# One masked product for the exponents of a decay matrix, in place of two products added in PSUM

## The chip, the cores and the metric

The kernel runs on one core of a Trainium2 chip. Its time is the device time of one execution in microseconds; the result is told as the median of several runs. TensorE (PE) multiplies matrices into PSUM, VectorE (DVE) and ScalarE (ACT) work element by element, GpSimd (POOL) and SyncE (SP) mostly issue DMAs. Each engine works through its own queue in order.

## What is computed

One layer of a hybrid trunk on 512 latent and 256 context tokens of width 2048: a modulated norm, one input projection, a Fourier head group beside a bidirectional state-space scan of 24 heads (four groups of six), an output projection and an MLP. The change touches the scan. Cut to it, the reference does this for each direction, chunk of 128 positions and head:

```python
acum = jnp.cumsum(dtc * a, axis=2)
seg = acum[:, :, :, None] - acum[:, :, None, :]
decay = jnp.exp(jnp.where(lower, seg, -jnp.inf))
cb = jnp.einsum('bclgn,bcsgn->bclsg', cc, bc)
y_diag = jnp.einsum('bclsgh,bcsghp->bclghp', decay * cb[..., None], xdt)
```

`seg` is the decay's exponent for a pair of positions l and s of one chunk: a term of l less a term of s.

## The kernel before

Everything lies in SBUF as 128 partitions by columns. Products of weights are made in three pieces (`mm3`, lines 106 to 108): a weight tile of 1024 columns is loaded by SP's queue, rounded to a high part by ScalarE (line 99), the rest is taken by VectorE (line 100), and high and low parts multiply 512 moving columns. Two such pairs of tiles (`whi`, `wlo`) exist.

The work goes in stages. Up to 153 us the first slab of the input projection runs beside the adaLN sums, whose weights come through five `araw` buffers. Then the set-up of the scan follows in the same stretch as the first group's projections: `dt_finish` makes the step sizes `dt`, `dta`, and lines 363 to 395 make from `dta` the cumulative sums that the scan needs, in two parts (a rounded one and its rest) so that products keep the precision. `pre` holds the sums for the factors of the states, `prm` the sums for the positions l (56 rows: head, and head again for the rest), and `pch` those for the positions s (112 rows: chunk and head, twice). The scratch tiles `scr` and `hs_` are taken from `araw`. `sel` and `selp` are constants that pick heads; they are loaded and cast after the first group's projections (lines 513 to 516).

Then come the Fourier group, the context tokens (to about 476 us), and from there to about 820 us the scan, `scan_group` four times. In each group `i` goes over three pairs of heads; one such pass is called a unit below, so there are twelve. A unit makes the states (line 631, then VectorE at 640), and for each of its two heads and two directions the exponents: `sg` gets the product of `sel` for the head with `prm` (line 654, 56 rows) and on top of it the product of `pch` with `sel` for the chunk (line 656, 112 rows). ScalarE turns it by Relu and Exp (lines 660, 661) into the decay, VectorE multiplies by B and C's product (662), and PE multiplies with x (667). The states' part follows with `selp` and `pre` (673, 675, 679 to 681), and at the end the gate, whose squares are ScalarE's (588, 591). Beside the units PE works on the projections of the next group (`lat_group`), for the last group on a part of z (`z_last`) and on the output projection.

What stands in which place of each queue is decided when the program is built: a scheduler takes the code's order, priorities (`load_split` has a high one) and free buffers, and writes a fixed order for each engine.

Of the kernel before, what the change touches and what calls it, by code (L numbers as in the profile page):

```python
# [14 lines left out]
P = 128  # L15
# [18 lines left out]
NSB = 14  # L34
SHARED = [(16 + k, 0) for k in range(2, 14)]
NZ1 = 9
N1P = 3
N1S = 2 * N1P

# [15 lines left out]
def tile_hybrid_trunk(ctx, tc, xT, ctxT, cvec, ccol, vec, alog, w_ada, w_adr, w_ins, w_zs, w_in, w_dt, w_f, w_o,  # L55
# [81 lines left out]
    def vcol(i):  # L137
        return vt[:, i:i + 1]
# [77 lines left out]
    na = smp.tile([P, 2 * NH], F32, name="na")  # L216


    pre = smp.tile([56, 2, L], F32R, name="pre")
    prm = smp.tile([56, 2, L], F32R, name="prm")  # L220
    pch = smp.tile([112, 2, 2, P], F32R, name="pch")
    sel = smp.tile([112, 72], F32R, name="sel")
    selp = smp.tile([56, 12, P], F32R, name="selp")

    w_stack = ExitStack()
    open_weights(w_stack, 3, 2)
# [69 lines left out]
    with tc.tile_pool(name="st", bufs=1, side="right") as st, tc.tile_pool(name="st2", bufs=2, side="right") as st2, \  # L296
            tc.tile_pool(name="st4", bufs=3, side="right") as st4:
        cl = st.tile([P, 2 * HALF], F32, name="cl")
        xr = st.tile([P, KT, L], F32, name="xr")

        def ada_k(k):
            for ch in (16 + k, k):
                for hf in range(2):
                    if (ch, hf) in SHARED:
                        ada_half(ara, ch, hf, (mod, part, cl), (modc, partc, ccl))
                    else:
                        ada_half(ara, ch, hf, (mod, part, cl))
# [24 lines left out]
        widths = [P, P, P, P, 48, P, P, P]  # L332
        for k in range(KT):
            w = raw_tile()[:, :SLAB_IN]
            nc.sync.dma_start(out=w, in_=w_ins[k])
            if k == 1:
                nc.sync.dma_start(out=cstt, in_=cst)
                nc.sync.dma_start(out=na, in_=alog)
            hi, lo = big_pair()
            xs_h.append((hi, lo))  # L340
            tmp = st4.tile([P, L], F32, name="mtmp")
            v.tensor_mul(xr[:, k], xr[:, k], rstd)
            s.activation(tmp, xr[:, k], AF.Identity, bias=mod[:, k:k + 1], scale=s1[:, k:k + 1])
            s.copy(hi, tmp)
            o = 0
            for a, n in zip(accs, widths):
                te.matmul(a[:n], w[:, o:o + n], tmp, start=k == 0, stop=k == KT - 1)  # L347
                o += n
            if k + 1 < KT:
                ada_k(k + 1)  # L350
            v.tensor_sub(lo, tmp, hi.bitcast(F32))
        xm = xs_h
        background(6)
        for i in range(4):
            u = st2.tile([P, L], F32, name="sr")
# [10 lines left out]
        v.memset(scr[:, :896], 0.0)  # L366
        hs_ = ara.tile([P, HALF], F32, name="araw").bitcast(F32R)
        lp = scr[:, 0:448].rearrange("p (d c h) -> p d c h", d=2, c=NCH)
        lc = scr[:, 448:896].rearrange("p (d f h) -> p d f h", d=2, f=2)
        for d in range(2):  # L370
            mask = k_le if d == 0 else k_ge
            for o in (0, 32):
                v.tensor_copy(lp[:, d, :, o:o + NH], dta[:, :NCH, d * NH:(d + 1) * NH])
            for f in range(2):
                for o in (0, 64):
                    v.tensor_copy(lc[:, d, f, o:o + 48].rearrange("p (c h) -> p c h", c=NCH),
                                  dta[:, :NCH, d * NH + f * 12:d * NH + f * 12 + 12])
            mid = scr[:, 896:1024]
            v.tensor_scalar(mid, mask, mask[:, 63 + d:64 + d], None, ALU.subtract)
            for dst, m in ((pre, mask), (prm, mid)):  # L380
                pp = bank()
                for c in range(NCH):
                    te.matmul(pp[:56, c * P:(c + 1) * P], lp[:, d, c], m, start=True, stop=True)
                hi = hs_[:, d * L:(d + 1) * L]
                s.copy(dst[0:32, d], pp[0:32, :])
                s.copy(hi[32:56], pp[32:56, :])
                v.tensor_sub(dst[32:56, d], pp[32:56, :], hi[32:56].bitcast(F32))
# [3 lines left out]
            hi = hs_[:, d * L:d * L + 2 * P]  # L391
            po = pch[:, d].rearrange("p f s -> p (f s)")
            s.copy(po[0:64], pg[0:64])
            s.copy(hi[64:112], pg[64:112])
            v.tensor_sub(po[64:112], pg[64:112], hi[64:112].bitcast(F32))

    gp_stack = ExitStack()
    gp1 = gp_stack.enter_context(tc.tile_pool(name="gp1", bufs=1, side="right"))
# [106 lines left out]
    with tc.tile_pool(name="fp", bufs=1, side="right") as fp, tc.tile_pool(name="fp2", bufs=1, side="right") as fp2:  # L505
        tb = fp.tile([P, 8, NL], F32, name="tb")
        cw = fp.tile([P, 2, P], F32, name="cw")
        wf = fp.tile([P, 4, P], F32, name="wf")
        nc.gpsimd.dma_start(out=cw, in_=cw_d)
        nc.gpsimd.dma_start(out=wf, in_=w_f)  # L510
        nc.gpsimd.dma_start(out=tb, in_=dft)
        nxt = lat_group(0, 4, ctx_stats)
        selr = raw_tile()[:112, :72]
        nc.sync.dma_start(out=selr, in_=sel_d)
        s.copy(sel, selr)
        s.copy(selp.rearrange("p j (h q) -> p (j h) q", q=64), selr[:56, :NH].unsqueeze(2).broadcast_to([56, NH, 64]))
# [89 lines left out]
    def scan_group(g, bT, b_tok, cT, xT_, x_tok):  # L606
# [13 lines left out]
        for i in range(3):  # L620
# [29 lines left out]
            for hh in range(2):  # L650
                h = h0 + hh
                for d in range(2):
                    sg = bank()
                    te.matmul(sg, sel[:56, h:h + 1].broadcast_to([56, P]), prm[:, d], start=True, stop=False)
                    j = 24 + (h % 12) * NCH
                    te.matmul(sg, pch[:, d, h // 12], sel[:, j:j + NCH].unsqueeze(2).broadcast_to([112, NCH, P]),
                              start=False, stop=True)
                    e = spe.tile([P, NCH, P], F32, name=f"e{d}")
                    ef = e.rearrange("p a b -> p (a b)")
                    s.activation(ef, sg, AF.Relu, scale=-1.0)  # L660
                    s.activation(ef, ef, AF.Exp, scale=-1.0)
                    v.tensor_mul(e, e, cbu if d == 0 else cbl)
                    ms.append(e)
# [470 lines left out]
```

## Time and profile before

| | |
|---|---|
| median of three runs | 2385.83 us (2382.52 to 2394.14) |
| the profiled execution | 2374.16 us, its span 2372.4 us |
| PE busy | 2262.6 us, 95% of the span |
| DVE busy | 1811.1 us, 76% |
| ACT busy | 1176.3 us, 50% |
| POOL busy | 285.7 us, 12% |

The span goes from the first instruction to the last. Busy shares are averages over stages with different limits, so the stage of the change is to be read by itself. Matmuls are pipelined: the busy time of one reaches into the next, and the distance of their starts tells what one costs in the queue. PEld is the load of the stationary operand, which may lie beside a running product. A wait names who ended the idle time of an engine.

### The profile page before, as it was taken

To read this page: it belongs to the slowest core of one execution; us is meant where nothing else is said; L and a number is where in the kernel's file an instruction comes from. 1 tells how busy PE (TensorE), PEld (TensorE's weight loads), DVE (VectorE), ACT (ScalarE), POOL (GpSimd) and SP (SyncE) were. 2 spreads that over 40 slices of the span, in tenths; PEclk is the share of its full clock that TensorE was granted. 3 is DMA by queue.
4 is the path that set the end of the run, shared out by engine and by line. 5 is a ranking of instruction groups with operands and counts; after the bars stand their busy time and mean duration, and the time that the engine had idled before them with its cause. 6 is when DMAs were issued, how large, how long until landed. Compare 5 with 4: busy or idle time off the path is not lost.

```text
span 2372.4 us, 38829 instructions
## 1 busy us (share of the span) xinstructions
PE 2262.6 (95%) x15242; PEld 2004.8 (85%) x15242; DVE 1811.1 (76%) x2551; ACT 1176.3 (50%) x1646; POOL 285.7 (12%) x375
## 2 busy tenths in 40 slices
PE   6999999999999999898999999999999999999996
PEld 2347789877777777698999989999999999999995
DVE  7978779987778677675666666666898887888778
ACT  4125245456555422254444545555665665566554
POOL 0000000000000000111101101111122222222210
PEclk9999999999999999999999999999999999999998
DMA  8988877823224499557888877777899999999993
GB/s 297 333 296 299 330 240 261 279 83 122 83 63 148 144 345 303 187 163 230 253 224 244 239 217 220 208 209 213 242 264 267 266 250 267 259 265 247 242 267 116
DMA packets 163456, 544.72 MB, mean 230 GB/s; under 512 B 19284, under 2 KB 20196, under 8 KB 163016
## 3 DMA queue, kind: packets, MB, share of 16 engines
q1 hardware_dynamic: 115624, 402.35, 49.6%
q0 software_dynamic: 46496, 137.79, 27.1%
q8 instruction: 119, 1.95, 0.3%
q10 hardware_dynamic: 1152, 2.10, 0.2%
q14 instruction: 65, 0.53, 0.1%
HBM read 479.24 MB, written 62.92 MB: 229 GB/s over the span
## 4 chain that ended last, share of the span: by engine, by line
PE 63%; DVE 15%; DMA 14%; issue 4%; ACT 3%; SPq 0%; DVEq 0%; POOL 0%; ACTq 0%; POOLq 0%
PE acc L107 10%; PE acc L108 10%; PE acc L106 9%; PE bank L107 8%; PE bank L106 8%; PE bank L108 8%; DMA araw<-in_w_ada_dram 5%; DMA wraw<-in_w_adr_dram 3%; DVE araw L172 3%; DVE wlo L100 2%; DVE wlo L85 2%; DMA araw<-in_w_adr_dram 2%; DMA wraw<-in_w_o_dram 1%; PE bank L347 1%; PE bank L667 1%
## 5 line engine op out<-in xcount | busy, mean ns | idle before, releaser
L85 DVE TENSOR_TENSOR wlo<-wraw,whi 128x1024 fp32r<-128x1024 f32 x427 | 519.4, 1221 | 224.0 <-ACT whi L84 221.1
L84 ACT CAST whi<-wraw 128x1024 fp32r<-128x1024 f32 x427 | 445.4, 1048 | 448.8 <-PE bank L108 158.4
L107 PE MATMUL bank<-chi,wlo 128*128 128x256 f32 (+1 forms) x2000 | 569.7, 285 | 6.1 <-DVE wlo L85 6.1
L106 PE MATMUL bank<-chi,whi 128*128 128x256 f32 (+1 forms) x2000 | 569.6, 285 | 1.1 <-DVE ca L1023 0.8
L108 PE MATMUL bank<-clo,whi 128*128 128x256 f32 (+1 forms) x2000 | 569.3, 285 | 0.0
L107 PE MATMUL acc<-chi,wlo 128*128 128x256 f32 (+1 forms) x1512 | 435.7, 288 | 21.7 <-DVE wlo L85 21.5
L106 PE MATMUL acc<-chi,whi 128*128 128x256 f32 (+1 forms) x1512 | 433.4, 287 | 7.3 <-ACT chi L830 6.7
L108 PE MATMUL acc<-clo,whi 128*128 128x256 f32 (+1 forms) x1512 | 433.7, 287 | 0.0
L107 PEld LDWEIGHTS bank<-chi,wlo 128*128 128x128 f32 x2000 | 384.5, 192 | 7.7 <-DVE wlo L85 6.7
L106 PEld LDWEIGHTS bank<-chi,whi 128*128 128x128 f32 x2000 | 384.5, 192 | 2.6 <-DVE ca L1023 1.3
L108 PEld LDWEIGHTS bank<-clo,whi 128*128 128x128 f32 x2000 | 384.5, 192 | 0.9
L107 PEld LDWEIGHTS acc<-chi,wlo 128*128 128x128 f32 x1512 | 293.6, 194 | 25.7 <-DVE wlo L85 24.3
L106 PEld LDWEIGHTS acc<-chi,whi 128*128 128x128 f32 x1512 | 293.1, 194 | 9.5 <-ACT chi L830 7.6
L107 PE MATMUL acc<-bh,wlo 128*128 128x512 f32 x720 | 286.2, 397 | 13.3 <-DVE wlo L100 13.3
L108 PEld LDWEIGHTS acc<-clo,whi 128*128 128x128 f32 x1512 | 293.5, 194 | 1.6 <-DVE clo L832 0.6
L106 PE MATMUL acc<-bh,whi 128*128 128x512 f32 x720 | 285.3, 397 | 1.1 <-ACT whi L99 1.1
L108 PE MATMUL acc<-bl,whi 128*128 128x512 f32 x720 | 284.4, 395 | 0.0
L99 ACT CAST whi<-wraw 128x1024 fp32r<-128x1024 f32 (+2 forms) x145 | 142.7, 987 | 263.3 <-PE acc L108 228.6
L867 POOL DMA_DIRECT2D wraw<-in_w_dram x122 | 105.1, 861 | 757.1 <-DMA wraw<-in_w_dram 334.8
L100 DVE TENSOR_TENSOR wlo<-wraw,whi 128x1024 fp32r<-128x1024 f32 (+2 forms) x145 | 165.6, 1144 | 29.0 <-ACT whi L99 28.0
L107 PEld LDWEIGHTS acc<-bh,wlo 128*128 128x128 f32 x720 | 136.1, 189 | 48.2 <-DVE wlo L100 20.1
L106 PEld LDWEIGHTS acc<-bh,whi 128*128 128x128 f32 x720 | 136.0, 189 | 29.8 <-ACT whi L99 1.6
(336 smaller groups left out, 3274.0 us busy)
## 6 DMA issues: line engine op xcount, KB each, us to landing
wraw<-in_w_dram SPq DMA_DIRECT2D x305, 512.0 KB, 5.2
araw<-in_w_ada_dram SPq DMA_DIRECT2D x164, 512.0 KB, 6.7
wraw<-in_w_dram POOLq DMA_DIRECT2D x122, 512.0 KB, 8.0
wraw<-in_w_in_dram SPq DMA_DIRECT2D x84, 512.0 KB, 4.5
x<-ca POOLq DMA_DIRECT2D x112, 256.0 KB, 8.0
araw<-in_w_adr_dram SPq DMA_DIRECT2D x48, 512.0 KB, 4.6
wraw<-in_w_adr_dram SPq DMA_DIRECT2D x32, 512.0 KB, 7.7
hid<-ct POOLq DMA_DIRECT2D x32, 512.0 KB, 5.4
```

Of the source, the lines that this page charges most:

```text
L84: s.copy(hi, raw)
L85: v.tensor_sub(lo, raw, hi.bitcast(F32))
L99: s.copy(hi, raw)
L100: v.tensor_sub(lo, raw, hi.bitcast(F32))
L106: te.matmul(ps, a[0], b[0], start=first, stop=False, skip_group_check=on)
L107: te.matmul(ps, a[1], b[0], start=False, stop=False, skip_group_check=on)
L108: te.matmul(ps, a[0], b[1], start=False, stop=last, skip_group_check=on)
L172: v.tensor_tensor_reduce(o, a, cond[:, hf * HALF:(hf + 1) * HALF], 1.0, last if hf else first, ALU.mult, ALU.add, dst[:, ch:ch + 1] if hf ...
L347: te.matmul(a[:n], w[:, o:o + n], tmp, start=k == 0, stop=k == KT - 1)
L667: te.matmul(py[hh * 64:hh * 64 + 64, c * P:(c + 1) * P], xd[d][:, c, hh], ms[2 * hh + d][:, c], start=c == 0 and d == 0, stop=c == NCH - 1 ...
L867: nc.gpsimd.dma_start(out=raw[n], in_=d, accum_op=ALU.add)
```

## The change

The two products become one of 128 rows. Its moving operand `mov` (128 x 512 for each direction and each twelve heads) holds the sums of the positions l for the twelve heads, in two parts, in rows 0 to 23, zeros up to row 31, and in rows 32 to 127 ones where a row's chunk is the column's. Its stationary operand has ones in the first 32 rows and the sums of the positions s in the other 96 (`sta`). For each head ScalarE multiplies `sta` by a column of `pick` that has 1, -1 or 0 per row and so leaves the rows of that head alone; that is the masked operand `sh`, of which there are two buffers. `prm` and `pch` go. `selp` goes too, and the 56 x 128 operand of line 673 is spread from `sel` in each unit (`two`). The constants are loaded in the set-up, through `araw`, and the set-up holds a second scratch tile `scr2`.

```diff
-            for dst, m in ((pre, mask), (prm, mid)):
-                pp = bank()
-                for c in range(NCH):
-                    te.matmul(pp[:56, c * P:(c + 1) * P], lp[:, d, c], m, start=True, stop=True)
...
             pg = bank()[:, :2 * P]
             for f in range(2):
-                te.matmul(pg[:112, f * P:(f + 1) * P], lc[:, d, f], mid, start=True, stop=True)
...
+                pm = bank()
+                for c in range(NCH):
+                    te.matmul(pm[:24, c * P:(c + 1) * P], lq[:, d, f, c], mid, start=True, stop=True)
+                s.copy(hi[:24], pm[:24])
+                v.scalar_tensor_tensor(mov[:24, d, f], hi[:24].bitcast(F32), pick[:24, 12:13], pm[:24],
+                                       ALU.mult, ALU.add)
+                te.matmul(pg[:, f * P:(f + 1) * P], lc[:, d, f], mid, start=True, stop=True)
+            s.copy(hi[:, :2 * P], pg)
...
+            s.copy(sta[:32, d], ones[:32].unsqueeze(1).broadcast_to([32, 2, P]))
...
+        selr = ara.tile([P, HALF], F32, name="araw")
+        nc.sync.dma_start(out=selr[:, :NSEL], in_=sel_d)
+        v.tensor_copy(pick[:, 0:13], selr[:, 24:37])
+        s.copy(mov.rearrange("p d f t -> p (d f) t"), selr[:, 37:NSEL].unsqueeze(1).broadcast_to([P, 4, L]))
+        s.copy(sel, selr[:56, :NH])
...
                     sg = bank()
-                    te.matmul(sg, sel[:56, h:h + 1].broadcast_to([56, P]), prm[:, d], start=True, stop=False)
-                    j = 24 + (h % 12) * NCH
-                    te.matmul(sg, pch[:, d, h // 12], sel[:, j:j + NCH].unsqueeze(2).broadcast_to([112, NCH, P]),
-                              start=False, stop=True)
+                    sh = sp2.tile([P, P], F32R, name="sh")
+                    s.activation(sh, sta[:, d, h // 12].bitcast(F32), AF.Copy, scale=pick[:, h % 12:h % 12 + 1])
+                    te.matmul(sg, sh, mov[:, d, h // 12], start=True, stop=True)
...
+            two = sp.tile([56, P], F32R, name="two")
+            s.copy(two.rearrange("p (h q) -> p h q", q=64),
+                   sel[:, h0:h0 + 2].bitcast(F32).unsqueeze(2).broadcast_to([56, 2, 64]))
             for d in range(2):
                 pb = bank()
-                te.matmul(pb, selp[:, g * 3 + i], pre[:, d], start=True, stop=True)
+                te.matmul(pb, two, pre[:, d], start=True, stop=True)
```

The scheduler also writes another order. Three places follow. The lines of the new program are some 10 to 15 higher: its line 667 is the new product, 666 the Copy that makes `sh`, 670 and 671 are Relu and Exp, 107 to 109 are `mm3`.

PE's queue in the third unit of the first group before, from the states' products on:

```order
L631 MATMUL bank<-xs,b_tok 128x128 x3
L654 MATMUL bank<-prm,sel 128x512
L656 MATMUL bank<-sel,pch 128x512
L654 MATMUL bank<-prm,sel 128x512
L656 MATMUL bank<-sel,pch 128x512
L654 MATMUL bank<-prm,sel 128x512
L656 MATMUL bank<-sel,pch 128x512
L654 MATMUL bank<-prm,sel 128x512
L656 MATMUL bank<-sel,pch 128x512
L106 MATMUL acc<-bh,whi 128x512
```

The same place in the new program, its beginning, and then the end of the 21 weight products that follow:

```order
L642 MATMUL bank<-xs,b_tok 128x128 x3
L667 MATMUL bank<-mov,sh 128x512 x2
L108 MATMUL acc<-bh,wlo 128x512
```

```order
L107 MATMUL acc<-bh,whi 128x512
L667 MATMUL bank<-mov,sh 128x512 x2
L677 MATMUL bank<-e_3969,xd_3947 64x128
L686 MATMUL bank<-pre,two 128x512
L692 MATMUL bank<-cT,hg 128x128
```

Eight products in a row have become two, then 21 weight products, then two.

ScalarE's queue in the same unit before (`e` are the decays), from the cast of the weight tile on:

```order
L99 CAST whi<-wraw 128x1024
L464 COPY cvr<-acc 128x512
L660 ACTIVATE e_3934<-bank 128x512
L660 ACTIVATE e_3941<-bank 128x512
L661 ACTIVATE e_3934<-e_3934 128x512
L661 ACTIVATE e_3941<-e_3941 128x512
L660 ACTIVATE e_3948<-bank 128x512
L660 ACTIVATE e_3955<-bank 128x512
```

And in the new program:

```order
L602 ACTIVATE ee<-xT_1184 128x512
L481 ACTIVATE xT_4296<-cvr,vt 128x512
L670 ACTIVATE e_3969<-bank 128x512
L670 ACTIVATE e_3977<-bank 128x512
L100 CAST whi<-wraw 128x1024
L671 ACT_TABLE_LOAD
L671 ACTIVATE e_3969<-e_3969 128x512
L671 ACTIVATE e_3977<-e_3977 128x512
L666 ACTIVATE sh<-sta,pick 128x128 x2
L670 ACTIVATE e_3985<-bank 128x512
```

The two `sh` for the unit's second head stand behind Relu, a weight cast, a table load and Exp of its first.

SP's queue in the set-up before:

```order
L98 DMA wraw<-in_w_in_dram 128x1024 x2
L168 DMA araw<-in_w_ada_dram 128x1024 x3
L98 DMA wraw<-in_w_in_dram 128x1024 x3
L168 DMA araw<-in_w_ada_dram 128x1024 x3
L410 DMA araw<-in_ctxT_dram 128x1024 x3
```

And in the new program:

```order
L99 DMA wraw<-in_w_in_dram 128x1024 x2
L169 DMA araw<-in_w_ada_dram 128x1024 x3
L368 DMA araw<-in_sel_d_dram 128x549
L99 DMA wraw<-in_w_in_dram 128x1024 x3
L169 DMA araw<-in_w_ada_dram 128x1024 x3
L425 DMA araw<-in_ctxT_dram 128x1024 x3
```

The load of the constants has moved from behind the first group's projections to the middle of the set-up.

## Rows read from the trace of the kernel before

**Rows 1.** Waits of PE, 480 to 800 us: total us, times, longest.
```profile
PE bank L610 <- ACT cT L476: 3.0, 3, 1.6
PE bank L631 <- DVE xs L627: 1.0, 1, 1.0
PE acc L107 <- DVE wlo L100: 0.3, 1, 0.3
```
**Rows 2.** Busy time of each engine by stretch: the scan, then the output projection.
```profile
core 0: us, PE busy (x) PEld busy (x) DVE busy (x) ACT busy (x) POOL busy (x), PEclk, DMA share, GB/s
458.00:820.00 362.00, 355.95 (x1864) 269.10 (x1863) 284.49 (x516) 196.15 (x283) 22.91 (x42) 0.99 0.34 106
...
820.00:1000.00 180.00, 163.16 (x698) 129.50 (x696) 119.73 (x167) 43.53 (x52) 9.77 (x19) 0.99 0.83 291
```
**Rows 3.** Timeline of PE in one unit: start us, duration, engine, line, tiles, shape.
```profile
523.94 0.50 PE L654 MATMUL bank<-prm,sel 56*128 56x512 f32 x1
524.37 0.48 PE L656 MATMUL bank<-sel,pch 112*128 112x512 f32 x1
524.78 0.49 PE L654 MATMUL bank<-prm,sel 56*128 56x512 f32 x1
...
527.20 0.40 PE L106 MATMUL acc<-bh,whi 128*128 128x512 f32 x1
...
529.03 0.39 PE L108 MATMUL acc<-bl,whi 128*128 128x512 f32 x1
```
**Rows 4.** Weight loads of line 654: duration ns min/median/max, first and last start.
```profile
L654 PEld LDWEIGHTS bank<-prm,sel x48: 182/182/183, 484.5 to 789.4; 56*128 56x128 f32 x48
```
**Rows 5.** ScalarE's groups and two single rows: count, busy us, mean ns, idle before.
```profile
L99 ACT CAST whi<-wraw 128x1024 fp32r<-128x1024 f32 x26 | 27.3, 1050 | 50.7 <-PE acc L108 50.5
...
L476 ACT ACT_TABLE_LOAD x11 | 14.1, 1283 | 3.7 <-DVE cT L475 2.9 <-DVE xT L475 0.7
...
L1025 ACT ACTIVATE sn<-bank,mod 128x256 f32<-128x256 f32 x64 | 30.0, 469 | 3.2 <-PE bank L108 3.1
...
224.75 0.26 ACT L515 CAST sel<-wraw 112x72 fp32r<-112x72 f32 x1
```
**Rows 6.** Timeline of ScalarE in the unit of rows 3.
```profile
524.89 0.60 ACT L660 ACTIVATE e<-bank 128x512 f32<-128x512 f32 x1
...
526.22 1.14 ACT L661 ACTIVATE e<-e 128x512 f32<-128x512 f32 x2
527.26 1.08 ACT L660 ACTIVATE e<-bank 128x512 f32<-128x512 f32 x2
528.21 1.16 ACT L661 ACTIVATE e<-e 128x512 f32<-128x512 f32 x2
```
**Rows 7.** The set-up: PE's waits from 140 us; timelines of SP, DVE, ACT, PE.
```profile
PE bank L267 <- DVE dta L264: 2.7, 1, 2.7
PE acc L107 <- DVE wlo L100: 1.3, 1, 1.3
...
177.66 1.50 SPq L168 DMA_DIRECT2D araw<-in_w_ada_dram  x3
188.08 3.96 SPq L410 DMA_DIRECT2D araw<-in_ctxT_dram  x3
...
170.37 1.22 DVE L100 TENSOR_TENSOR wlo<-wraw,whi 128x1024 fp32r<-128x1024 f32 x1
...
190.39 1.28 DVE L172 CUSTOM_DVE_ANT_0 araw<-araw,ccl,vt 128x1024 f32<-128x1024 f32 x1
...
225.62 1.47 ACT L516 CAST selp<-wraw 56x1536 fp32r<-56x1536 f32 x1
...
186.35 1.08 PE L383 MATMUL bank<-araw 128*56 128x128 f32 x8
```
**Rows 8.** SP's queue at the scan's end: first load of adaLN weights behind it.
```profile
814.51 0.90 SPq L168 DMA_DIRECT2D araw<-in_w_ada_dram  x2
```

More of the change, by code (lines that the diff above doesn't have):

```diff
@@ L36 @@
 NZ1 = 9
+NSEL = 37 + L
 N1P = 3
@@ L219, in tile_hybrid_trunk @@
     pre = smp.tile([56, 2, L], F32R, name="pre")
[L220 to L223, printed above, removed]
+    mov = smp.tile([P, 2, 2, L], F32R, name="mov")
+    sta = smp.tile([P, 2, 2, P], F32R, name="sta")
+    pick = smp.tile([P, 16], F32, name="pick")
+    sel = smp.tile([56, NH], F32R, name="sel")
     w_stack = ExitStack()
@@ L364, in tile_hybrid_trunk @@
         dt_finish(accs[4][:48], L, 0, st)
+        selr = ara.tile([P, HALF], F32, name="araw")
[3 more added lines that the diff above has]
+        s.copy(sel, selr[:56, :NH])
         scr = ara.tile([P, HALF], F32, name="araw")
-        v.memset(scr[:, :896], 0.0)
+        v.memset(scr[:, :960], 0.0)
+        scr2 = ara.tile([P, HALF], F32, name="araw")
         hs_ = ara.tile([P, HALF], F32, name="araw").bitcast(F32R)
         lp = scr[:, 0:448].rearrange("p (d c h) -> p d c h", d=2, c=NCH)
-        lc = scr[:, 448:896].rearrange("p (d f h) -> p d f h", d=2, f=2)
+        lc = scr[:, 448:960].rearrange("p (d f h) -> p d f h", d=2, f=2)
+        lq = scr2[:, 0:384].rearrange("p (d f c h) -> p d f c h", d=2, f=2, c=NCH)
         for d in range(2):
@@ L374, in tile_hybrid_trunk @@
             for f in range(2):
[L375 to L378, printed above, removed]
-            v.tensor_scalar(mid, mask, mask[:, 63 + d:64 + d], None, ALU.subtract)
-            for dst, m in ((pre, mask), (prm, mid)):
-                pp = bank()
-                for c in range(NCH):
-                    te.matmul(pp[:56, c * P:(c + 1) * P], lp[:, d, c], m, start=True, stop=True)
[L384 to L387, printed above, removed]
+                hd = slice(d * NH + f * 12, d * NH + f * 12 + 12)
@@ new lines, in tile_hybrid_trunk @@
+                for o in (32, 80):
+                    v.tensor_copy(lc[:, d, f, o:o + 48].rearrange("p (c h) -> p c h", c=NCH), dta[:, :NCH, hd])
+                for o in (0, 12):
+                    v.tensor_copy(lq[:, d, f, :, o:o + 12], dta[:, :NCH, hd])
+            mid = scr2[:, 384:512]
+            v.tensor_scalar(mid, mask, mask[:, 63 + d:64 + d], None, ALU.subtract)
+            pp = bank()
+            for c in range(NCH):
+                te.matmul(pp[:56, c * P:(c + 1) * P], lp[:, d, c], mask, start=True, stop=True)
@@ L388, in tile_hybrid_trunk @@
+            hi = hs_[:, d * L:(d + 1) * L]
+            s.copy(pre[0:32, d], pp[0:32, :])
+            s.copy(hi[32:56], pp[32:56, :])
+            v.tensor_sub(pre[32:56, d], pp[32:56, :], hi[32:56].bitcast(F32))
             pg = bank()[:, :2 * P]
             for f in range(2):
-                te.matmul(pg[:112, f * P:(f + 1) * P], lc[:, d, f], mid, start=True, stop=True)
-            hi = hs_[:, d * L:d * L + 2 * P]
-            po = pch[:, d].rearrange("p f s -> p (f s)")
-            s.copy(po[0:64], pg[0:64])
@@ L394, in tile_hybrid_trunk @@
-            s.copy(hi[64:112], pg[64:112])
-            v.tensor_sub(po[64:112], pg[64:112], hi[64:112].bitcast(F32))
+                pm = bank()
+                for c in range(NCH):
+                    te.matmul(pm[:24, c * P:(c + 1) * P], lq[:, d, f, c], mid, start=True, stop=True)
[3 more added lines that the diff above has]
+                te.matmul(pg[:, f * P:(f + 1) * P], lc[:, d, f], mid, start=True, stop=True)
@@ L397, in tile_hybrid_trunk @@
+            s.copy(hi[:, :2 * P], pg)
+            so = sta[:, d].rearrange("p f s -> p (f s)")
+            v.scalar_tensor_tensor(so, hi[:, :2 * P].bitcast(F32), pick[:, 12:13], pg, ALU.mult, ALU.add)
+            s.copy(sta[:32, d], ones[:32].unsqueeze(1).broadcast_to([32, 2, P]))
     gp_stack = ExitStack()
@@ L512, in tile_hybrid_trunk @@
         nxt = lat_group(0, 4, ctx_stats)
[L513 to L516, printed above, removed]
         for g in range(4):
@@ L1104 @@
     cst = np.ascontiguousarray(np.concatenate([k_ == s_, k_ < e_, k_ >= e_], 1).astype(f))
-    sel_d = np.zeros((112, 72), f)
+    sel_d = np.zeros((P, NSEL), f)
     for h in range(NH):
@@ L1108 @@
     for h in range(12):
+        sel_d[[h, 12 + h], 24 + h] = 1.0
         for c in range(NCH):
-            sel_d[[c * 12 + h, 64 + c * 12 + h], 24 + h * NCH + c] = -1.0
+            sel_d[[32 + c * 12 + h, 80 + c * 12 + h], 24 + h] = -1.0
+            sel_d[[32 + c * 12 + h, 80 + c * 12 + h], 37 + c * P:37 + (c + 1) * P] = 1.0
+    sel_d[12:24, 36] = -1.0
+    sel_d[80:128, 36] = -1.0
     t = np.arange(L)
```

## The prediction

> **What bounds the kernel now.** I first asked where the removed products run. They all lie between 484 and 790 us, in the scan of the four head groups, so that stretch decides and the rest of the span only has to pass the gain on. I read the waits of TensorE there: in 320 us it waits 4.3 us for anybody, 3.0 of them three times at line 610 for the last convolution of a group [rows 1]. In the stretch table PE is busy 356 of 362 us, VectorE 284 and ScalarE 196, with the DMA engines at 0.34 [rows 2]. So the scan is bound by TensorE's own queue, VectorE is the next (0.79), and ScalarE, which gets the new work, has 166 us free. What leaves PE's queue there shortens the kernel, as long as what replaces it on ScalarE is in time.
>
> Next I read the timeline of one unit (a pair of heads; three in a group, twelve in all). Busy times of PE overlap, so starts are to be used. The eight old products start 0.42 us apart, from 523.94 to the 527.20 at which the weight products go on: 3.26 us. The products of lines 106 to 108 behind them have the same 512 columns and start 0.23 us apart (527.20 to 529.03 in eight steps) [rows 3]. No wait stands there. The difference, 0.19 us, is the length of the old product's own weight load, 182 ns [rows 4]: beside products of 128 rows the load lies hidden, and in this alternation of 56 and 112 rows it doesn't.
>
> **1. The products.** Removed: 12 units x 3.26 us = 39.1 us of PE's queue. Added: 48 products with 128 rows, 128 columns and 512 moving columns, the shape of lines 106 to 108, with such products or line 631's 128-row ones around them: 48 x 0.23 = 11.0 us. Balance **-28.1 us**. The old products wait for nothing, so there is no stall in this number that could reappear.
>
> One rule of the Trainium skill reads otherwise. Its page "TensorE: Matmul & The Clock Gate", section "Step-by-step: what each phase is for", says that the time of a weight load goes by its columns, that the row count K doesn't matter, and that loads are pulled ahead of running products where row groups don't conflict or the background buffer is free. By the first half alone 56 and 112 rows would cost nothing and the 0.42 us would have another cause, which the new product might keep (rival B). The trace doesn't settle it: the loads are indeed of one length, but they stand open there.
>
> **2. The masked operand on ScalarE.** Each product needs `sh` first: a Copy of 128x128 with a scale per partition, 48 of them, and twelve `two` casts of 56x128. No such row exists. Nearest are the 128x256 Copy with a column of scales, 469 ns, and the 112x72 cast, 0.26 us [rows 5]; I take 0.36 us, near the middle, 17 us for the 48 and 20 with `two`. ScalarE has room for that. What matters is the order: `sh` has two buffers, so the queue on PE is now two products, 21 to 11 weight products, two products; and on ScalarE the second two `sh` stand behind both Relus and both Exps of the first two. PE waits behind them with all its weight products.
>
> The chain of a unit by rows [rows 5, 6]: first product's end 0.40, 0.04 to the Relu (as 524.85 to 524.89), two Relus 0.95 (527.26 to 528.21), table load 1.28, two Exps 1.04 (526.22 to 527.26), the cast of the next weight tile that stands among them 1.05, two `sh` 0.65: 5.4 us. PE has 2 + 21 starts of 0.23 us = 5.3 us until the third product. So stands it in units 1 to 7 (one of them with 19 for 21 and an earlier `sh`). In units 8 and 9 there is no table load and 15 products (4.1 against 3.9), in unit 10 no cast and 17 (4.4 against 4.4), in the last two neither and 11 (3.1 against 3.0). PE would wait some 0.1 us in each unit, under 2 us in all. The third product's load can't lie under anything when its operand comes late: 12 x 0.19 = 2.3 us. With a little for a ScalarE that isn't free when the first product ends I take **+5 us**. Lower end 0; upper end 15, when ScalarE comes to the Relus 1.2 us late in each unit. That is about one weight cast (1.05 us), and those wait for PE 50.5 us in this stretch [rows 5], so the queue can come late.
>
> For the first two `sh` of a unit the cover is what stands between two units: 23 or more weight products, over 5 us. They are issued behind the Exps of line 675 and wait for nothing but a free buffer.
>
> **3. The set-up.** It lies at 160 to 200 us, where PE waits 2.7 us for `dta` and 1.3 us for a weight tile [rows 7]. PE gets 28 small products for 20, two passes each at 0.13 us (eight instructions of line 383 take 1.08 us [rows 7]): +2 us. VectorE gets eight small copies more. ScalarE loses the 1.47 us cast of `selp` [rows 7] and gets the one of `mov`, a third longer, behind the first of three weight casts; the next weight subtraction waits for PE's release until 170.4 us anyway [rows 7], which covers it. SP's queue: the load of `sel_d` moves ahead of three weight loads and of the next loads of adaLN weights, and the set-up now holds four of the five `araw` buffers for two. One adaLN load that was issued near 178 us must then wait for the buffer of `scr`, until near 188 us, and the three loads of `ctxT` behind it, which go out at 188 us now, come with it [rows 7]; VectorE reached such tiles only after 190 us. The three uses of each half of `hs_` now follow each other, and weight casts stand behind them. I take **+3 us**: lower end -1 (two weight triples now stand ahead of the wait for `dta`), upper end 8.
>
> **4. Behind the scan.** The next stage, the output projection, is near the DMA's limit (0.83 over 820 to 1000 us [rows 2]). It still takes the gain, because its loads of adaLN weights first go out at 814.51 us [rows 8], when the scan's memory is free, and move with the end of the scan. The scheduler writes this stage in another order (three `w_1s` loads stand behind, not before, the first adaLN loads), same loads: 0, ends -4 and +4.
>
> **The sum** is -28.1 + 5 + 3 + 0 = **-20 us**: the profiled execution would go from 2374.2 to 2354 us. Its time is 11.7 us under the median of the three runs, 2385.8, from which I forecast: **2366 us**. All ends together give -33 and -1.
>
> **Rivals.**
> A, ScalarE becomes the pace of the unit: the squares of lines 588 and 591 stand before the Relus in six units and wait for VectorE, which at 284 of some 339 us would be 0.84 busy. At the upper end of 2, 15 us, it leaves -10: 2376 us. For it: the chain and PE's cover are equal within 0.2 us. Against it: ScalarE begins the Relu 0.04 us behind the product now. Chance 0.15.
> B, the open load stays with the new product (0.42 us each): 48 x (0.815 - 0.42) = 19.0 us saved, with 8 of cost -11: 2375 us. This is the rule named under 1. Against it: 0.23 us in all products of this shape. Chance 0.08.
> C, slower: in nine units a weight cast stands between the Relus and `sh`. If its tile comes late from memory, `sh` waits with it and PE behind `sh`, where PE had finished all eight products before. A whole tile's time, 24 x 0.23 = 5.5 us, in nine units is 50 us: -28 + 50 + 3 = +25, 2411 us. It decides against the change from 2.8 us per unit. Against it: of the casts' 50.7 us idle, 50.5 are PE's release [rows 5], at a DMA share of 0.34. Chance 0.04.
> D, the stage behind swallows it: if its end hung on transfers that don't move with the scan, or if the new order costs what the scan gives, no change, 2385 us. Chance 0.07. That the change doesn't do what it says I give nothing: the new program has 48 products for 96.
>
> **How the numbers follow.** Forecast 0.66. Two in ten may stay outside: 2353 (all lower ends) to 2384 (all upper ends but a last us) holds the forecast, A and B, and leaves C and most of D out. A measurement here can tell some 0.5%, 12 us, so faster begins below 2374: nine tenths of the forecast and a third of A and B, 0.67. Slower is C and a trace of D, 0.05. The rest, 0.28, is the same.
>
> **What would show it.** The new product's starts 0.23 us apart and the first pair without a wait (step 1; 0.42 is B). PE's waits in the scan: a new row "product <- sh" of 2 to 5 us in all is step 2, 15 or more is A, and single waits of several us behind a weight cast is C. The scan's stretch should shrink from 362 us to some 339, with the group starts about 6 us closer. The first scan product at 484.5 us should come 0 to 6 us later (step 3); the stretch from the scan's end to 1000 us should keep its 180 us (step 4), else D.

## The result, and the profile after

The changed kernel takes 2359.9 us in the median of four runs (2356.7 to 2361.9) against 2385.4 of before (2382.5 to 2394.1): ratio 0.9883, 95% interval 0.9857 to 0.9909. Six further runs gave 2361.5 us, ratio 0.9900 (0.9881 to 0.9920). By the two intervals together it is 19 to 34 us faster; the forecast was 20 us less, 2366, range 2353 to 2384.

The two profiled executions stand closer, 2361.6 after against 2374.2 before. The profile of before was a short execution: a second one, taken for the experiments, took 2382.9 us. So I give both wherever before and after are compared.

Stretches of the scan and of the output projection, after (answering to [rows 2]; the columns are as there):

```profile
core 0: us, PE busy (x) PEld busy (x) DVE busy (x) ACT busy (x) POOL busy (x), PEclk, DMA share, GB/s
458.00:796.00 338.00, 333.23 (x1851) 262.65 (x1850) 286.90 (x522) 211.34 (x345) 22.35 (x41) 1.00 0.37 119
800.00:980.00 180.00, 161.36 (x671) 127.58 (x669) 117.72 (x164) 42.92 (x51) 9.72 (x18) 0.96 0.83 287
```

PE is still busy nearly all the time (333 of 338 us), ScalarE has 15 us more than in the old stretch of 362 us, and the stage behind has its old numbers but for the granted clock, 0.96 for 0.99; its length is the old one (table below). The new operand and its product (duration ns min/median/max, first and last start; then who waited how long, how often, and the longest wait), answering to [rows 4]:

```profile
L666 ACT ACTIVATE sh<-sta,pick x48: 385/391/405, 469.5 to 768.5; 128x128 fp32r<-128x128 f32 x48
L667 PEld LDWEIGHTS bank<-mov,sh x48: 186/190/192, 491.3 to 768.9; 128*128 128x128 f32 x48
L667 PE MATMUL bank<-mov,sh x48: 392/458/506, 491.3 to 769.0; 128*128 128x512 f32 x48
...
PEld bank L667 <- ACT sh L666: 3.3, 13, 0.3
```

The 3.3 us are waits of the load queue (PEld). The waits of PE itself from 484 to 780 us, answering to [rows 1], have none for `sh`:

```profile
PE bank L621 <- ACT cT L491: 1.1, 2, 0.9
PE bank L642 <- issue: 1.1, 1, 1.1
PE bank L642 <- DVE xs L638: 1.0, 1, 1.0
```

And one unit on PE, the first of the scan, answering to [rows 3]. The 21 weight products between the two pairs are left out but for the first and the last:

```profile
491.33 0.71 PE L667 MATMUL bank<-mov,sh 128*128 128x512 f32 x2
491.88 0.40 PE L107 MATMUL acc<-bh,whi 128*128 128x512 f32 x1
...
496.46 0.39 PE L109 MATMUL acc<-bl,whi 128*128 128x512 f32 x1
496.70 0.79 PE L667 MATMUL bank<-mov,sh 128*128 128x512 f32 x2
497.42 0.43 PE L677 MATMUL bank<-e,xd 128*64 128x128 f32 x2
```

The first pair holds the queue for 491.33 to 491.88, 0.55 us, the second for 496.70 to 497.42, 0.72 us: 1.27 us where the eight products of a unit took 3.26 [rows 3].

Where the time went, by the first and last start of the exponents' first product, the first start of the product behind the scan's stage (line 776, after 789) and that of VectorE's last line (1051, after 1064), in us:

| | scan, first to last | its length | from its last to line 776 | from there to line 1051 |
|---|---|---|---|---|
| before, first execution | 484.5 to 789.4 | 304.9 | 205.5 | 1363.7 |
| before, second | 488.4 to 790.2 | 301.8 | 207.6 | 1369.6 |
| after, first | 491.3 to 769.0 | 277.7 | 206.4 | 1370.7 |
| after, second | 492.2 to 770.2 | 278.0 | 207.9 | 1365.8 |

The whole gain is in the scan: 25.5 us between the means. The scan begins 3 to 8 us later, 5.3 between the means. Behind it the change leaves no mark that these executions can tell: both kernels lie in the same 206 to 208 and 1364 to 1371 us.

By these four executions the change is worth 18 us (25.5 less 5.3, and less 2.2 behind the scan), and their times say the same, 2378.5 and 2360.5 in the mean. The medians of all runs have 24 to 26. Both profiled executions of before were shorter than the median of its runs, and no profile shows in which stretch the 6 to 8 us between lie.

### The profile page after: what moved, and what is told of

The parts are those of the page before. It is cut to its first block, busy times and chain, and to the rows that moved or that the text cites. A ratio compares the mean times of both kernels' runs of the same rounds, so it can differ in the third digit from the quotient of the medians.

```text
span 2359.8 us, 38865 instructions
## 1 busy us (share of the span) xinstructions
PE 2241.0 (95%) x15210; PEld 1997.3 (85%) x15210; DVE 1812.6 (77%) x2562; ACT 1189.8 (50%) x1706; POOL 285.7 (12%) x375
## 4 chain that ended last, share of the span: by engine, by line
PE 66%; DMA 14%; DVE 13%; issue 4%; ACT 2%; SPq 0%; DVEq 0%; POOL 0%; ACTq 0%; POOLq 0%
PE acc L108 11%; PE acc L109 10%; PE acc L107 10%; PE bank L108 9%; PE bank L107 9%; PE bank L109 9%; DMA araw<-in_w_ada_dram 5%; DMA wraw<-in_w_adr_dram 4%; DVE araw L173 3%; DVE wlo L101 2%; DMA araw<-in_w_adr_dram 2%; DVE wlo L86 2%; PE bank L349 1%; PE bank L677 1%; PE bank L692 1%
## 5 line engine op out<-in xcount | busy, mean ns | idle before, releaser
L100 ACT CAST whi<-wraw 128x1024 fp32r<-128x1024 f32 (+3 forms) x145 | 142.9, 988 | 245.5 <-PE acc L109 204.8
L101 DVE TENSOR_TENSOR wlo<-wraw,whi 128x1024 fp32r<-128x1024 f32 (+3 forms) x145 | 165.7, 1145 | 35.8 <-ACT whi L100 35.5
```

Source lines behind the costliest of these rows:

```text
L100: s.copy(hi, raw)
L101: v.tensor_sub(lo, raw, hi.bitcast(F32))
```

## The experiments

The theory: the old pairs held PE mostly because their weight loads lay open in the alternation of 56 and 112 rows. The rivals: the loads are open for another reason, ScalarE's new work costs more than it shows (A), the later start of the scan is the price of the set-up's new load and cast. The runs came in three groups, each with its own runs of before (medians 2385.4, 2385.5, 2385.3).

**The changed kernel again.**

> The changed kernel again, unaltered, on the chip of the three runs beside it; its profile is a second execution to set against the first. My account: 25 to 28 us less than before (the timed runs so far had 2360 against 2385), the first product of the scan again 5 to 8 us later than the 484.5 of before, the scan again 27 to 28 us shorter from its first product to its last, and the rest from the scan's end to the kernel's end in its old length. If the 7 us by which the stretch from the main projections to the end was longer in the profile of after than in the profile of before is a cost of the change, this execution shows it again; if it is only how two executions differ, it moves by several us.

2361.5 us (2359.4 to 2366.7), 23.9 under before where 25 to 28 were expected. The scan came 7.7 us later than in the first profile of before and took 278.0 us, as expected. In the MLP, from ScalarE's first step of line 929 (942 after) to the last transfer that line 1045 issues (1058 after), the first profile of after was 7 us longer than that of before (1173.3 against 1166.3 us); this shrank to 2.8 (1169.1).

**The old pair with equal row counts.** Before's kernel, both products kept, operands filled up with zeros:

```diff
-    prm = smp.tile([56, 2, L], F32R, name="prm")
-    pch = smp.tile([112, 2, 2, P], F32R, name="pch")
-    sel = smp.tile([112, 72], F32R, name="sel")
+    prm = smp.tile([P, 2, L], F32R, name="prm")
+    pch = smp.tile([P, 2, 2, P], F32R, name="pch")
+    sel = smp.tile([P, 72], F32R, name="sel")
...
-    te.matmul(sg, sel[:56, h:h + 1].broadcast_to([56, P]), prm[:, d], start=True, stop=False)
+    te.matmul(sg, sel[:, h:h + 1].broadcast_to([P, P]), prm[:, d], start=True, stop=False)
```

> The kernel before with both products of a pair kept, but both operands of 56 and of 112 rows filled up to 128 rows with zeros (three copies more in the set-up, the same sums). It takes away nothing but the changes of row count. My account (the 0.42 us between the old products comes from a weight load of 182 ns that lies open because the products alternate between 56 and 112 rows, and equal shapes follow one another at 0.23): the pair takes 0.46 us in place of 0.81, so 48 x 0.35 = 17 us less than before, about 2369, without any product removed. Rival (the row count is not what opens the load; it is the load from a broadcast column, or the switch from an even older operand, which this edit leaves as it was): the spacing stays at 0.42 and the time at that of before, within 3 us. In between, if only one of the two loads is hidden: 8 to 9 us less.

2362.3 us (2358.3 to 2370.0), ratio 0.9903 (0.9878 to 0.9928): as fast as the changed kernel, with nothing removed. PE in a unit of this run:

```profile
503.79 0.48 PE L656 MATMUL bank<-prm,sel 128*128 128x512 f32 x1
504.10 0.38 PE L658 MATMUL bank<-sel,pch 128*128 128x512 f32 x1
504.32 0.39 PE L656 MATMUL bank<-prm,sel 128*128 128x512 f32 x1
504.55 0.38 PE L658 MATMUL bank<-sel,pch 128*128 128x512 f32 x1
...
505.44 0.38 PE L658 MATMUL bank<-sel,pch 128*128 128x512 f32 x1
505.65 0.39 PE L108 MATMUL acc<-bl,whi 128*128 128x512 f32 x1
```

Starts 0.23 us apart, but for the first; eight products in 1.86 us (503.79 to 505.65) in place of 3.26. Twelve units give 12 x 1.40 = 16.8 us, as expected. The scan shrank by 18 to 21 us (to 283.9), and the time by 23, where 17 were expected; the interval has 17 to 29, and no profile places the rest.

**112 rows for both.** Only the first product is filled up, from 56 to 112:

```diff
-    te.matmul(sg, sel[:56, h:h + 1].broadcast_to([56, P]), prm[:, d], start=True, stop=False)
+    te.matmul(sg, sel[:, h:h + 1].broadcast_to([112, P]), prm[:, d], start=True, stop=False)
```

> The kernel before with the first product of a pair filled up with zeros from 56 to 112 rows, so that both products of a pair have 112 rows; the products around them keep 128. With 128 rows for both, the products stood 0.23 us apart and the kernel was 23 us faster than before, with nothing removed. Theory 1 (the load of a weight is hidden if the product before it has the same number of rows): inside a group of pairs the spacing falls to 0.23, only the steps into and out of the group keep 0.41, and the time is 12 to 18 us less than before. Theory 2 (it takes all 128 rows, equal or not): the spacing stays at 0.41 and the time within 3 us of before.

2362.4 us (2360.4 to 2364.8), 23 under before, more than the 12 to 18 of theory 1. The end of a group on PE:

```profile
507.93 0.39 PE L655 MATMUL bank<-prm,sel 112*128 112x512 f32 x1
508.16 0.38 PE L657 MATMUL bank<-sel,pch 112*128 112x512 f32 x1
508.37 0.40 PE L108 MATMUL acc<-bl,whi 128*128 128x512 f32 x1
```

0.23 us apart, so theory 2 falls. But the step out of the group, from 112 to 128 rows, takes 0.21 us where theory 1 had 0.41: 112 beside 128 doesn't open the load either, which is why this run gained more than theory 1 had. It is the 56 rows beside more.

**56 rows alone.** Before's kernel without the second product:

```diff
-    te.matmul(sg, sel[:56, h:h + 1].broadcast_to([56, P]), prm[:, d], start=True, stop=False)
-    j = 24 + (h % 12) * NCH
-    te.matmul(sg, pch[:, d, h // 12], sel[:, j:j + NCH].unsqueeze(2).broadcast_to([112, NCH, P]),
-              start=False, stop=True)
+    te.matmul(sg, sel[:56, h:h + 1].broadcast_to([56, P]), prm[:, d], start=True, stop=True)
```

> The kernel before without the second product of each pair (its term is left out of the exponents), so that the 48 products of 56 rows follow one another in groups of up to four, with products of 128 rows around the group. Theory 1 (a load lies open where the row count steps between 56 and 112 or 128): inside a group the products stand 0.23 us apart, only the steps into and out of the group stay at 0.41, and the time is 48 x 0.83 = 40 us less than before, less about 2 x 12 x 0.2 = 5 us for the steps and 48 x 0.23 = 11 for the products that stay: 2359 to 2364. Theory 2 (a load or product of 56 rows is slow by itself, whatever stands next to it): the spacing inside the group stays at 0.41, and the time is 48 x 0.18 = 8 us more than that, 2367 or more.

2358.2 us (2348.5 to 2359.3), just under the 2359 to 2364 of theory 1. The last two products of 56 rows of a group of four, the weight product behind them (each row from a window of its own):

```profile
507.38 0.39 PE L654 MATMUL bank<-prm,sel 56*128 56x512 f32 x1
...
507.61 0.39 PE L654 MATMUL bank<-prm,sel 56*128 56x512 f32 x1
...
507.94 0.50 PE L106 MATMUL acc<-bh,whi 128*128 128x512 f32 x1
508.27 0.39 PE L107 MATMUL acc<-bh,wlo 128*128 128x512 f32 x1
```

56 behind 56 is 0.23 us, 128 behind 56 is 0.33, and the next again 0.33. So 56 rows aren't slow by themselves (theory 2 falls); the step is.

**The changed kernel without the masked copies.**

```diff
-    s.activation(sh, sta[:, d, h // 12].bitcast(F32), AF.Copy, scale=pick[:, h % 12:h % 12 + 1])
-    te.matmul(sg, sh, mov[:, d, h // 12], start=True, stop=True)
+    te.matmul(sg, sta[:, d, h // 12], mov[:, d, h // 12], start=True, stop=True)
```

> The changed kernel without its masking: the product of a head takes the operand common to its twelve heads as it stands, so the 48 masked copies on ScalarE, 0.39 us each, and every wait for them are gone, and the exponents are the sums over twelve heads (this part of the computation is left out). My account (the copies lie beside other work of TensorE, and cost 3.3 us of waits and a little push on the work behind them): 3 to 6 us less than the changed kernel. Rival A of the prediction (ScalarE sets the pace of a unit, so its 48 x 0.39 = 18.8 us lie on the path): 12 us less or more. If ScalarE has room everywhere: within 2 us.

2360.6 us (2352.4 to 2368.1), 0.9 under the changed kernel: no difference in the time that these runs can tell. In its profile the scan took 272.2 us for 278.0 (497.2 to 769.4), so the copies cost some 6 us there. That execution was the slowest of the four and started its scan late. Rival A, 12 us or more, doesn't show in either number.

**Each masked copy twice.** The line that makes `sh` stands twice:

```diff
+    s.activation(sh, sta[:, d, h // 12].bitcast(F32), AF.Copy, scale=pick[:, h % 12:h % 12 + 1])
```

> The changed kernel with each masked copy on ScalarE made twice, one after the other into the same buffer: 48 copies of 0.39 us more, 18.8 us of ScalarE, and the result as it was. My account (ScalarE is busy 211 of 338 us in the scan, and the copies lie beside other work of TensorE): 2 to 6 us more than the changed kernel, and the waits of TensorE for the copy, 3.3 us, grow to 5 to 9. Rival A (ScalarE sets the pace of a unit): 15 us more or nearly so. If there is room everywhere: within 2 us.

2361.2 us (2351.7 to 2368.8): no more than the changed kernel, where my account had 2 to 6 us. The scan took 281.8 us, 3.8 more, for 18.8 us more of ScalarE. The waits for the copy:

```profile
PEld bank L668 <- ACT sh L667: 3.9, 12, 0.8
```

3.9 us for 3.3, less than my account had. Rival A falls: a fifth of the added work came through to the scan, none that can be told to the time.

**The table's load and casts further ahead**, in the second step of the first projection slab, where the cast runs at 37.7 us (not beside the context projections, as my text has it):

```diff
+                selr = ara.tile([P, HALF], F32, name="araw")
+                nc.sync.dma_start(out=selr[:, :NSEL], in_=sel_d)
+                v.tensor_copy(pick[:, 0:13], selr[:, 24:37])
+                s.copy(mov.rearrange("p d f t -> p (d f) t"), selr[:, 37:NSEL].unsqueeze(1).broadcast_to([P, 4, L]))
+                s.copy(sel, selr[:56, :NH])
```

(and the same lines taken out of the set-up)

> The changed kernel with the load of the 0/1 table and the three casts out of it (the large one takes 1.92 us on ScalarE and stood there 4.89 us waiting for its load) placed further ahead in the set-up, beside the context projections, where ScalarE waits for other loads anyway. My account (that wait of ScalarE held up the next weight cast, and with it TensorE and the adaLN load on SyncE's queue, and cost the scan's start some 4 to 7 us): the first product of the scan 3 to 6 us earlier than in the changed kernel, and the time 4 to 6 us less. Rival (the later start comes from the longer chain of products, subtractions and copies itself, or is covered further on by the load of weights, which sets the pace there): within 2 us of the changed kernel.

2358.8 us (2357.5 to 2363.4), 2.7 less than the changed kernel, not to be told from no difference. ScalarE's wait for the load was 0.36 us there and gone from the set-up, but the first product of the scan came at 495.1 us, later and not earlier. My account of the late start fell.

**The table's load and the casts in before's kernel**, as dead work:

```diff
+        selr = ara.tile([P, HALF], F32, name="araw")
+        nc.sync.dma_start(out=selr[:, :NSEL], in_=sel_d)
+        mov = ara.tile([P, HALF], F32, name="araw").bitcast(F32R)
+        for _ in range(2):
+            s.copy(mov.rearrange("p (d t) -> p d t", t=L), selr[:, 37:NSEL].unsqueeze(1).broadcast_to([P, HALF // L, L]))
```

> The kernel before with the load of the larger 0/1 table (281 KB) and two dead casts of 128x1024 out of it put where the changed kernel has its load and its cast of 128x2048; nothing else is changed, the pairs stay. In the profiles so far the scan's first product came at 484 to 489 us with the old set-up and at 491 to 497 with the new one, also where load and casts stood further ahead. Theory 1 (the load and the cast, in the queues of SyncE and ScalarE, are the cost): first product at 491 or later, and 4 to 7 us more than before. Theory 2 (it is the rest: two products more a head group, the longer chain behind them, and the order in which the work around them comes out): first product at 484 to 489, and the time within 3 us of before.

2385.9 us against 2385.3, ratio 1.0004 (0.9988 to 1.0021), first product at 489.0: theory 2. ScalarE stood there nearly as long for the load as in the changed kernel (4.47 for 4.89 us):

```profile
169.07 1.05 ACT L370 CAST araw<-araw 128x1024 fp32r<-128x1024 f32 x1 [4.47 <-DMA araw<-in_sel_d_dram]
```

**Before again.**

> The kernel before again, unaltered. Its profile is a second execution of before, since the first one (2374 us) lay under all timed runs of before (2382 to 2394). My account: no difference in the time, within 3 us; the scan 304 to 306 us from its first product to its last as in the first profile, and the stretch from the second dense layer's first product to the last product of line 1045, 1166 us in the first profile, nearer to the 1169 to 1173 of the changed kernel, so that nothing of the gain was lost there. If it is again 1166, the changed kernel does lose 3 to 7 us behind the scan.

2386.0 us, ratio 1.0002 (0.9982 to 1.0022). The scan took 301.8 us, 2 under the lower end of what I had written, and the stretch behind 1173.2 us, so the 1166.3 of the first profile was that execution's own and no gain was lost there.

**The remaining operands of 56 rows filled up**, in the changed kernel and in before's. My text there names line 677 and 675; the 24 products stand in line 686 after, 673 before.

```diff
-    pre = smp.tile([56, 2, L], F32R, name="pre")
+    pre = smp.tile([P, 2, L], F32R, name="pre")
...
-            two = sp.tile([56, P], F32R, name="two")
+            two = sp.tile([P, P], F32R, name="two")
```

> The changed kernel with the operands of the last products that have 56 rows (the decay at the chunk's start, 24 in the scan, line 677) filled up to 128 rows with zeros; nothing is removed. By the 0.36 us that a product of the old pair gave back when its rows were filled up, counted for the load before it and the load behind it (0.18 each): 24 x 0.18 to 0.36 = 4 to 9 us less than the changed kernel, 2352 to 2357. If these 24 products stand where TensorE waits for ScalarE or VectorE anyway, as their neighbours of 0.43 us among the products of 64 columns would allow: within 2 us of the changed kernel.

> The kernel before with all three operands of 56 or 112 rows filled up to 128 rows: the two of each pair, and those of the 24 products of line 675. Both products of a pair stay. By the same sum as for the changed kernel with its 24 products filled up: 4 to 9 us less than the 2362 that the pair alone gave, 2353 to 2358. Theory that the changed kernel's gain is only the row counts: no slower than the changed kernel filled up, within 3 us. Theory that removing a product is worth something of its own (48 x 0.23 = 11 us of TensorE, less 3 us of waits and 5 us of later start): the changed kernel filled up is 3 us faster or more.

The changed kernel filled up takes 2353.0 us (2349.8 to 2360.0), ratio to before 0.9864 (0.9842 to 0.9886), 8.5 less than unfilled. Before filled up takes 2358.3 us (2352.6 to 2365.0), ratio 0.9883 (0.9860 to 0.9907), 4 less than with the pair alone. Each of these intervals still meets that of its unfilled kernel, the first only just, so the starts below have to carry the claim. The scans shrank by 6.1 and 6.6 us. In the changed kernel, such a product and its neighbours before the filling (in its second execution):

```profile
518.39 0.49 PE L686 MATMUL bank<-pre,two 56*128 56x512 f32 x1
518.82 0.49 PE L692 MATMUL bank<-cT,hg 128*128 128x128 f32 x2
519.14 0.83 PE L692 MATMUL bank<-cT,hs 128*128 128x128 f32 x6
```

and with it:

```profile
521.00 0.51 PE L687 MATMUL bank<-pre,two 128*128 128x512 f32 x1
521.35 0.38 PE L693 MATMUL bank<-cT,hg 128*128 128x128 f32 x2
521.57 0.83 PE L693 MATMUL bank<-cT,hs 128*128 128x128 f32 x6
```

From the product to line 692's second group it is 0.75 us without (518.39 to 519.14) and 0.57 with (521.00 to 521.57): 0.18 us a product, 24 x 0.18 = 4.3 us, the lower end of what was expected and most of the scan's gain. Between the two filled-up kernels lie 5.3 us in favour of the single product, with intervals that overlap.

**Both, filled up and ahead.**

> The changed kernel with the operands of line 677's 24 products filled up to 128 rows, which gave 8 us, and with the table's load and casts further ahead in the set-up, which gave 3 us at most and left the scan's start where it was. If the two add up: 2348 to 2352. If the place of load and casts is worth nothing, as the late start of the scan in that run says: 2351 to 2355, the time of the filled-up kernel within 2 us.

2351.7 us (2349.9 to 2355.1), ratio 0.9857 (0.9840 to 0.9874), 1.3 under the filled-up kernel: not to be told apart, so the place of the load is worth nothing that shows. It has the lowest median of all kernels here, 33.6 us under before, and its interval lies clear of that of the changed kernel in its second set (0.9881 to 0.9920).

## Why the prediction was right, step by step

**What bounds the kernel** held. What left PE's queue in the scan shortened the kernel, and the stage behind passed it on.

**1, the products: held, and for the reason given.** The loads of the old pairs lay open because of their row counts: with equal counts the same 96 products stand 0.23 us apart. Rival B, by which the row count doesn't matter, falls for the spacing. The loads last 182 to 190 ns in the median whatever the rows. That agrees with the Trainium skill's page "TensorE: Matmul & The Clock Gate", section "Step-by-step: what each phase is for", by which a load's time goes by its columns and not by its rows. But whether a load lies hidden hung here on its rows and on those of the product ahead. What the prediction didn't draw from this is that the 28 us aren't the price of the second product. Of 39.1 us, 96 x 0.23 = 22 were the products and 17 the open loads, and the 17 were to be had by filling up with zeros.

**2, the masked operand: held in size, by luck, for its parts were off.** The copy took 391 ns, not 360. The Trainium skill's page "ScalarE: Activation LUTs", section "What ACT_TABLE_LOAD costs", gives 186 ns, 0.833 ns a column and 93 ns for a pointer operand, by which an estimate would have been 386. I had PE wait under 2 us for it, and 2.3 us of open loads. PE itself waits for no copy: in all twelve units the third product starts 0.22 to 0.27 us behind the weight product ahead of it (496.46 to 496.70 in the unit above). The 3.3 us are the load queue's, and reach PE only as open loads. A unit's two pairs held the queue for 0.55 and 0.72 us, not 0.46 each, so 12 x 0.35 = 4.2 us lay open where I had 2.3: the first pair loses as well. That makes 4.2 for the 5 taken; without the copies the scan was 5.8 us shorter. The products and the operand together were -23 in the sum. By the starts, 12 x (3.26 - 1.27) = 23.9 us left PE's queue, its waits in the scan fell by 1 (from 4.3 [rows 1] to 3.2), and the scan's length came out at -24 to -27.

**3, the set-up: +3 was said, 3 to 8 measured, and its mechanism was only in part the one I wrote.** I had let the cast of `mov` be covered by the weight subtraction's wait for PE [rows 7]. ScalarE's timeline after:

```profile
163.72 1.04 ACT L100 CAST whi<-wraw 128x1024 fp32r<-128x1024 f32 x1
169.64 1.92 ACT L370 CAST mov<-araw 128x2048 fp32r<-128x2048 f32 x1 [4.89 <-DMA araw<-in_sel_d_dram]
171.46 1.04 ACT L100 CAST whi<-wraw 128x1024 fp32r<-128x1024 f32 x1
```

The cast stood 4.89 us for its own load, which I had not counted, and the subtraction behind came at 172.53 us instead of 170.37 [rows 7]. SP's queue was held as forecast, with the adaLN loads blocked from 178.38 us and `ctxT` behind them at 189.98 for 188.08 [rows 7]:

```profile
178.38 10.94 SPq L169 DMA_DIRECT2D araw<-in_w_ada_dram  x3
189.98 4.47 SPq L425 DMA_DIRECT2D araw<-in_ctxT_dram  x3
```

But the load and its casts don't settle the scan's start. Before with this load and its casts as dead work starts it at 489.0 us, beside 484.5 and 488.4 without; the changed kernel without that wait starts it at 495.1, beside 491.3 and 492.2 with it. Over all runs, the old set-up gave 484.5 to 489.0 (seven kernels or executions) and the new one 491.3 to 497.2 (seven). So the set-up does cost, 5 us between the medians of the two.

The traces say where. At the first product of the Fourier group (line 442, 457 after) 4.7 of the 5 us are there already, between the medians: it starts at 235.6 to 237.7 us in the seven of the old set-up, at 238.1 to 243.5 in the seven of the new. Between 160 and 245 us two things differ. The small products of the set-up hold PE longer; before, then after, from the first of them to the weight product behind the last:

```profile
181.45 1.96 PE L383 MATMUL bank<-cstt,araw 128*56 128x128 f32 x8
...
187.80 0.48 PE L108 MATMUL acc<-bl,whi 128*128 128x512 f32 x1
```

```profile
180.84 1.96 PE L393 MATMUL bank<-cstt,araw 128*56 128x128 f32 x8
...
189.88 0.50 PE L108 MATMUL acc<-bh,wlo 128*128 128x512 f32 x1
```

That is 9.0 us after and 5.9 before (without a weight product that stands between); over the seven of each kind the medians are 8.7 and 6.0, so the +2 that I had for these products was nearly +3. And PE waits more: 6.4 to 8.3 us in all for 4.1 to 5.7, medians 7.0 and 5.0. One of these waits is for `zs`, which ScalarE makes from the later `ctxT`, 1.3 to 2.0 us for 1.1 at most. The prediction had asked only when VectorE reaches such tiles; ScalarE reads `ctxT` too, and here it waits for it:

```profile
195.91 0.72 ACT L429 ACTIVATE zs<-araw 128x256 f32<-128x256 f32 x2 [1.42 <-DMA araw<-in_ctxT_dram]
```

So the added products and the later `ctxT`, both in my text, are what the traces show, and not the cast of `mov`. No run takes either away by itself, and how much the scheduler's new order adds stays open.

**4, behind the scan: held**, 206 to 208 us from the scan's last product to line 776's first in all four executions.

**The sum** was -20. It came out at -24 to -26 in the medians and at -18 between the means of the profiled executions. The scan gave 2 to 3 us more than forecast and its later start took 2 more, so two errors offset each other, which is luck; what else parts the two figures is the spread of the executions, which no row places. The base held as well. I forecast from the median and not from the profiled execution, and the second profile of before shows that the first was 9 us short. Rival C, weight casts late from memory, shows nowhere: no wait for a copy was longer than 0.3 us. Rival D falls by step 4.

## What to carry to other kernels

Where products in a row have different numbers of rows, look at the distance of their starts before you remove any of them. If it is longer than that of full products by a weight load, fill the short operands up with zeros: here that gave 23 us, where the change gave 24 to 26, without taking a product away, and by the starts 4 more in a place where the change hadn't looked. A gain that comes out as forecast doesn't show that its cause is the edit itself; the run that undoes the edit and keeps the suspected cause does.

## What the runs showed of the hardware

Starts of products of 512 columns, by the rows of the product and of the one ahead: 56 behind 56, 0.23 us; 112 behind 112, 0.23; 128 behind 112, 0.21; 112 behind 56 and 56 behind 112, 0.41 to 0.43 [rows 3]; 128 behind 56, 0.33.

Two of these can mislead. A product whose load lay open is recorded 0.48 to 0.50 us long, for 0.38 to 0.40, and the next start comes 0.1 us later than it would. So in before's unit 128 behind 112 takes 0.32 (to 527.20 [rows 3]), because the product of 112 rows there stands behind one of 56:

```profile
526.88 0.48 PE L656 MATMUL bank<-sel,pch 112*128 112x512 f32 x1
```

And 128 behind 56 costs 0.1 us ahead and 0.1 behind, 0.2 in all, about one load of 0.19. The open part isn't the unequal number as such, since 112 and 128 go together. The Trainium skill's page "TensorE: Matmul & The Clock Gate" states in "Architectural detail: the array is 16× 32×32, not 1× 128×128" that row groups go in strips of 32. By that, 112 and 128 rows use the same four strips and 56 rows two, which would fit all five; no run here tried 96 rows or 64 beside 128, so this stays a guess.

Two executions of the same program differed by 4 us in when the scan began and by 7 us in the MLP (1166.3 and 1173.2 us), so one pair of profiles shows a cost of a few us only in the stretch of the change itself.
